# Down projections by Strassen's seven products between the up projections of a two-layer decoder trunk

## The chip, the cores and the metric

The kernel runs on one core of one Trainium2 chip. The metric is the device time of one execution in microseconds. The profiler gives one more execution, with the time of every instruction on every engine: TensorE (PE, and PEld for its weight loads), VectorE (DVE), ScalarE (ACT), GpSimd (POOL) and SyncE (SP, which here only issues transfers).

## The reference

A decoder trunk of two layers on 512 tokens of width 1024, in float32. Layer 0 has retention and stick-breaking attention, layer 1 differential attention. Behind each of them comes the part that this case is about, a gated MLP with a causal convolution of width 3 over the tokens:

```python
def conv_ffn(x, w_up, conv_w, conv_b, w_down):
    S = x.shape[1]
    h = x @ w_up                                   # 512 x 1024 by 1024 x 5632
    hp = jnp.pad(h, ((0, 0), (CONV_W - 1, 0), (0, 0)))
    h = sum(hp[:, j:j + S] * conv_w[j] for j in range(CONV_W)) + conv_b
    u, g = jnp.split(h, 2, axis=-1)
    return (jax.nn.silu(g) * u) @ w_down           # 512 x 2816 by 2816 x 1024
...
        f = conv_ffn(x, w_up[l], conv_w[l], conv_b[l], w_down[l])
        x = layer_norm(ALPHA * x + f, ln2_g[l], ln2_b[l])
```

## The kernel before

**Three matmuls for one.** Every float32 operand is kept as a pair of float32r tiles, a rounded one (`h`) and the rest (`l`). `mm3` (L138 to L142) computes h.h, h.l and l.h into one PSUM bank, so each 128 x 128 by 128 x 512 block product is three matmuls.

**Weights.** `wload` (L123) takes a chunk of 128 x 2048 values (1 MB): a transfer issued by SP into a `raw` tile (L126), two ScalarE copies of 1024 columns that round to `h` (L133) and two VectorE subtractions that leave `l` (L135). There are two raw buffers, and in the MLP five pairs of weight tiles in a ring (three of pool `w`, two of `ffnw`). `chunk` hands out the next chunk and calls for those `ahead` of it.

**The MLP of one layer** (`ffn`, L382). Of 5632 columns of `w_up`, 128 of u and the matching 128 of g are one chunk. An up projection is 2 x 8 x 3 = 48 matmuls into two banks, one for u and one for g, both [128 columns, 512 tokens]. `conv` (L396) then does the convolution: one ScalarE instruction (L400) and two VectorE ones (L402) per bank, SiLU on ScalarE (L407), the product u.g on VectorE (L408), and `act_split` (L328, L329) makes the pair of operand tiles of that block. There are 22 blocks per layer. The down projection takes them in groups of 8, 8 and 6 (`FFN_GROUPS`). The first two groups each run as one section: for each half of the 1024 output columns and each of four token blocks, 8 x 3 = 24 matmuls into one bank, which VectorE folds into the residual x (L468 in the first group, L471 in the second). The last group's banks go to the layer norm (`LayerNorm.add`, L918).

**PSUM** has eight banks: in the MLP six take matmul sums in turn (three of `mmps`, three of `mmps2`), two (`trps`) take transposes.

**Order.** TensorE runs its instructions in the order in which the program writes them. On the other engines, SP among them, a list scheduler sets the order when the program is built, and each engine then works its queue in that order. The last chunks of one stage and the first of the next share the ring. In the attention stages the order of TensorE's work is written out by hand (`EVEN_SEQ`, `EVEN_CUTS` and their like).

## Time and profile before

| | |
|---|---|
| Time, median of 3 runs | 1249.89 us (1249.67 to 1249.92) |
| Profiled execution, first to last instruction (its span) | 1247.3 us |
| Busy on TensorE, matmuls | 1223.3 us, 5972 matmuls |
| Busy on VectorE | 746.8 us, 1172 instructions |
| Busy on ScalarE | 543.0 us, 830 instructions |
| Busy on GpSimd | 84.7 us, 142 instructions |
| Moved by transfers | 123.34 MB, mean 99 GB/s |

The profile gives the span of its execution; what lies around the span is not listed apart. The profile's page lists, in order, the busy time of each engine, the span in 40 slices, the transfer queues, the chain of work that ended last, the costliest groups of instructions and the transfers issued. Other views of the same trace list instructions in order of time, who waited for whom, and busy times by stretch. L126 is line 126 of the kernel.

### The profile page before, as it was taken

The page shows a single profiled execution, that of the slowest core. Times are in us where ns is not written, and L with a number is a line of the kernel's source. Part 1 is how long each engine was busy: PE and PEld are TensorE (multiplying, and loading weights), DVE is VectorE, ACT ScalarE, POOL GpSimd, SP SyncE. Part 2 cuts the span into 40 slices and gives each one's busy share as a digit, 9 for nine tenths or more (in the row PEclk, how much of TensorE's full clock was granted, in tenths as well). Part 3 has the DMA queues.
Part 4 walks back from the last instruction along what each step waited for, and adds up shares of the span by engine and source line. Part 5 has one row for each costly group of instructions (what it writes and reads, how often), then busy time and mean ns, then how long its engine had stood idle before and what let it go on. Part 6 is the DMA issues. An engine that isn't in the chain of part 4 may idle for free.

```text
span 1247.3 us, 14937 instructions
## 1 busy us (share of the span) xinstructions
PE 1223.3 (98%) x5972; PEld 1014.0 (81%) x5972; DVE 746.8 (60%) x1172; ACT 543.0 (44%) x830; POOL 84.7 (7%) x142
## 2 busy tenths in 40 slices
PE   8999998999999999999999999999999999999997
PEld 6888877888888888888888888787988888888886
DVE  5866688796553466335565658777765445543544
ACT  5454565445441344223235658764544224422321
POOL 0211122110000000000000001011000000000000
PEclk9999999999999999999999999999999999999999
DMA  8322121243222222222152213222422132221201
GB/s 316 124 102 76 43 89 64 90 169 128 84 99 101 102 101 101 80 90 101 37 165 102 75 52 111 85 75 107 169 102 101 68 135 90 81 100 68 101 1 68
DMA packets 23565, 123.34 MB, mean 99 GB/s; under 512 B 3318, under 2 KB 4127, under 8 KB 10952
## 3 DMA queue, kind: packets, MB, share of 16 engines
q1 hardware_dynamic: 23496, 122.39, 27.6%
q8 instruction: 47, 0.77, 0.2%
q14 instruction: 22, 0.18, 0.0%
HBM read 120.26 MB, written 4.74 MB: 100 GB/s over the span
## 4 chain that ended last, share of the span: by engine, by line
PE 86%; DVE 6%; ACT 4%; issue 1%; POOL 1%; DMA 1%; POOLq 0%; DVEq 0%; ACTq 0%
PE mmps L141 26%; PE mmps L140 26%; PE mmps L142 26%; DVE wl L135 2%; PE dacc L837 1%; DVE t L586 1%; PE dz L321 1%; PE dz L320 1%; DVE t L584 1%; PE wtr L827 1%; PE sbacc L616 1%; PE mmps L650 1%; PE xtp L955 1%; ACT wh L133 1%; POOL zp L589 1%
## 5 line engine op out<-in xcount | busy, mean ns | idle before, releaser
L140 PE MATMUL mmps<-xTh,wh 128*128 128x512 f32 (+1 forms) x1008 | 384.5, 381 | 5.0 <-ACT wh L201 4.5
L141 PE MATMUL mmps<-xTl,wh 128*128 128x512 f32 (+1 forms) x1008 | 380.8, 378 | 0.8 <-DVE xTl L958 0.8
L142 PE MATMUL mmps<-xTh,wl 128*128 128x512 f32 (+1 forms) x1008 | 379.3, 376 | 0.5 <-DVE wl L135 0.5
L135 DVE TENSOR_TENSOR wl<-raw,wh 128x1024 fp32r<-128x1024 f32 x196 | 242.9, 1256 | 172.5 <-ACT wh L133 172.2
L133 ACT CAST wh<-raw 128x1024 fp32r<-128x1024 f32 x196 | 200.6, 1046 | 255.4 <-PE mmps L141 173.1
L140 PEld LDWEIGHTS mmps<-xTh,wh 128*128 128x128 f32 x1008 | 189.9, 188 | 39.7 <-ACT wh L201 4.5
L142 PEld LDWEIGHTS mmps<-xTh,wl 128*128 128x128 f32 x1008 | 189.7, 188 | 36.9 <-DVE wl L135 1.0
L141 PEld LDWEIGHTS mmps<-xTl,wh 128*128 128x128 f32 x1008 | 190.0, 188 | 33.6 <-DVE xTl L958 1.5
L140 PE MATMUL mmps<-wh,acth 128*128 128x512 f32 x480 | 191.1, 398 | 0.2
L141 PE MATMUL mmps<-wl,acth 128*128 128x512 f32 x480 | 188.2, 392 | 0.0
L142 PE MATMUL mmps<-wh,actl 128*128 128x512 f32 x480 | 188.0, 392 | 0.0
L402 DVE SCALAR_TENSOR_TENSOR cvt<-mmps,cv,cvt 128x511 f32<-128x511 f32 (+1 forms) x176 | 130.9, 745 | 40.2 <-ACT cvt L400 39.7
L140 PEld LDWEIGHTS mmps<-wh,acth 128*128 128x128 f32 x480 | 90.1, 188 | 21.2 <-DVE x L255 0.7
L142 PEld LDWEIGHTS mmps<-wh,actl 128*128 128x128 f32 x480 | 90.0, 188 | 21.0 <-DVE actl L332 0.5
L141 PEld LDWEIGHTS mmps<-wl,acth 128*128 128x128 f32 x480 | 90.1, 188 | 18.4
L400 ACT ACTIVATE cvt<-mmps,cv 128x512 f32<-128x512 f32 x88 | 68.3, 776 | 43.6 <-PE mmps L142 43.4
L407 ACT ACTIVATE cvt<-cvt 128x512 f32<-128x512 f32 x44 | 27.8, 632 | 85.9 <-DVE cvt L402 85.9
L140 PE MATMUL mmps<-wh,xTh 128*128 128x512 f32 x160 | 64.9, 406 | 0.0
L142 PE MATMUL mmps<-wh,xTl 128*128 128x512 f32 x160 | 62.6, 391 | 0.0
L141 PE MATMUL mmps<-wl,xTh 128*128 128x512 f32 x160 | 62.4, 390 | 0.0
L935 POOL TENSOR_SCALAR lst<-lst 128x1 f32<-128x1 f32 x16 | 7.1, 445 | 778.9 <-ACT junk L931 778.9
L328 ACT CAST acth<-cvt 128x512 fp32r<-128x512 f32 x44 | 26.9, 611 | 63.4 <-PE mmps L141 60.3
(142 smaller groups left out, 1163.7 us busy)
## 6 DMA issues: line engine op xcount, KB each, us to landing
raw<-in_w_up SPq DMA_DIRECT2D x44, 1024.0 KB, 4.8
raw<-in_w_down SPq DMA_DIRECT2D x22, 1024.0 KB, 4.8
raw<-in_w_ot SPq DMA_DIRECT2D x8, 1024.0 KB, 5.1
raw<-in_w_et SPq DMA_DIRECT2D x6, 1024.0 KB, 4.8
raw<-in_w_en SPq DMA_DIRECT2D x6, 1024.0 KB, 5.1
raw<-in_w_oe SPq DMA_DIRECT2D x4, 1024.0 KB, 5.4
raw<-in_w_on SPq DMA_DIRECT2D x4, 1024.0 KB, 4.8
raw<-in_w_oo SPq DMA_DIRECT2D x4, 1024.0 KB, 4.7
```

The costliest lines, as they stand in the source:

```text
L133: nc.scalar.copy(h[:, sl], raw[:, sl])
L135: nc.vector.tensor_tensor(l[:, sl], raw[:, sl], h[:, sl].bitcast(F32), op=ALU.subtract)
L140: mm(out, lh, rh, start=start, stop=False)
L141: mm(out, lh, rl, start=False, stop=False)
L142: mm(out, ll, rh, start=False, stop=stop)
L320: self.nc.tensor.matmul(out, lhs, B[:, m, 0:n], start=True, stop=False)
L321: self.nc.tensor.matmul(out, lhs, B[:, 2 + m, 0:n], start=False, stop=True)
L328: nc.scalar.copy(h, src)
L400: nc.scalar.activation(t, ps, AF.Identity, bias=cv[:, f, 3:4], scale=cv[:, f, 2:3])
L402: nc.vector.scalar_tensor_tensor(out=t[:, d:], in0=ps[:, :S - d], scalar=cv[:, f, c:c + 1], in1=t[:, d:], op0=ALU.mult, op1=ALU.add)
L407: nc.scalar.activation(g, g, AF.Silu)
L584: nc.vector.scalar_tensor_tensor(out=t, in0=zp, scalar=0.0, in1=t, op0=ALU.max, op1=ALU.add)
```

## The change

The first 16 blocks of a layer are taken in four groups of four. A group's part of the down projection is [512 tokens x 512] by [512 x 1024]. Each operand is cut into 2 x 2 parts (256 tokens by 256 of the inner dimension; 256 of the inner dimension by 512 columns), and the eight part products become seven, m1 to m7, each 2 token blocks x 2 x 3 = 12 matmuls of 512 columns. Four products need sums of two, three or four parts of the weights: SP loads the first part into the raw tile, and GpSimd issues transfers that add the others to it in memory. The sums of activations are four GpSimd subtractions of 256 columns per pair of blocks (`quad_operands`). The products stand between the next group's up projections (`SLOTS`): m1 and m2 behind the first, m5 and m6, m3 and m7, m4. Each sum stays in a PSUM bank to which the next product adds, and VectorE folds it into x, with either sign, at each step. The last six blocks stay as they were.

For this the weights of the whole kernel are handled in units of 1024 columns (512 KB) instead of 2048: four raw buffers (five in the MLP), six pairs of weight tiles (eight in the MLP). The MLP's up projections get four PSUM banks instead of six; the other two hold sums of the products, and two more of these lie in the banks of the transposes.

```diff
-FFN_GROUPS = ((0, 8), (8, 8), (16, 6))
+UNIT = 1024
+QUADS = 4
+LAST0 = 4 * QUADS
+LASTN = NPAIR - LAST0
+SUMS = {"m1": ("11",), "m2": ("21",), "m5": ("11", "12"), "m6": ("11", "12", "22"), "m3": ("22",), "m7": ("12", "22"),
+        "m4": ("11", "12", "21", "22")}
+BLOCKS = ("11", "12", "21", "22")
+SLOTS = (("m1", "m2"), ("m5", "m6"), ("m3", "m7"), ("m4",))
...
+    def unit(self, srcs):
+
         nc = self.nc
-        raw = self.rawp.tile([P, 2048], F32, tag="raw", name=self.nm("raw"))
-        nc.sync.dma_start(out=raw, in_=src)
+        raw = self.rawpools[self.ri % len(self.rawpools)].tile([P, UNIT], F32, tag="raw", name=self.nm("raw"))
+        self.ri += 1
+        nc.sync.dma_start(out=raw, in_=srcs[0])
+        for src in srcs[1:]:
+            nc.gpsimd.dma_start(out=raw, in_=src, accum_op=ALU.add)
+        h, l = self.unit_tiles()
+        nc.scalar.copy(h, raw)
+        nc.vector.tensor_tensor(l, raw, h.bitcast(F32), op=ALU.subtract)
+        return h, l
...
+    def unit_tiles(self):
         wp = self.wpools[self.wi % len(self.wpools)]
         self.wi += 1
-        h = wp.tile([P, 2048], F32R, tag="wh", name=self.nm("wh"))
-        l = wp.tile([P, 2048], F32R, tag="wl", name=self.nm("wl"))
-        halves = (slice(0, 1024), slice(1024, 2048))
-        for sl in halves:
-            nc.scalar.copy(h[:, sl], raw[:, sl])
-        for sl in halves:
-            nc.vector.tensor_tensor(l[:, sl], raw[:, sl], h[:, sl].bitcast(F32), op=ALU.subtract)
-        return h, l
-
-    def mm3(self, out, lh, ll, rh, rl, start, stop):
+        return (wp.tile([P, UNIT], F32R, tag="wh", name=self.nm("wh")),
+                wp.tile([P, UNIT], F32R, tag="wl", name=self.nm("wl")))
...
-        while self.csrc and len(self.cget) < ahead:
+        while self.csrc and sum(len(c.units) for c in self.cget.values()) < ahead:
             k = self.csrc.pop(0)
             self.cget[k] = self.wsrc(k)
 
     def wsrc(self, key):
+        if key[0] == "w_sum":
+            _, l, g, name = key
+            return Chunk([self.unit([self.a["w_quad"][l][g][BLOCKS.index(b)] for b in SUMS[name]])])
...
-        return self.wload(src)
+        return Chunk([self.unit([src[:, o:o + UNIT]]) for o in (0, UNIT)])
...
-        self.rawp = P_("raw", 2)
-        self.wp = P_("w", 3)
+        self.rawp = P_("raw", 4)
+        self.wp = P_("w", 6)
...
-            ps2 = c2.enter_context(self.pool(f"mmps2_{l}", 3, space=PSUM))
+            ps2 = c2.enter_context(self.pool(f"mmps2_{l}", 1, space=PSUM))
             tp = c2.enter_context(self.pool(f"ffnt_{l}", 2))
             cp = c2.enter_context(self.pool(f"ffnc_{l}", 1))
             w2 = c2.enter_context(self.pool(f"ffnw_{l}", 2))
+            act2 = c2.enter_context(self.pool(f"ffna_{l}", 4))
+            raw2 = c2.enter_context(self.pool(f"ffnr_{l}", 1))
             cv = cp.tile([P, 2 * NPAIR, 4], F32, tag="cv", name=self.nm("cv"))
             nc.sync.dma_start(out=cv, in_=self.a["conv"][l])
-            self.mmpools = [(self.mmps1, "mm"), (ps2, "mm2")]
-            self.wpools = [self.wp, w2, self.wp, w2, self.wp]
-            self.wi = 0
-            acts = {}
+            self.mmpools = [(self.mmps1, "mm")] * 3 + [(ps2, "mm2")]
+            self.mmi = 0
+            self.wpools = [self.wp, self.wp, self.wp, w2] * 2
+            self.rawpools = [self.rawp] * 4 + [raw2]
+            self.wi = self.ri = 0
+            acts, firsts, ops = {}, {}, {}
+            t1, t2 = slice(0, 256), slice(256, S)
+
+            def quad_operands(g, kk, u, v):
+
+                q = tp.tile([P, 4, 256], F32, tag="q", name=self.nm("q"), bufs=1)
+                sub = nc.gpsimd.tensor_tensor
+                sub(q[:, 0], u[:, t2], v[:, t2], op=ALU.subtract)
+                sub(q[:, 3], u[:, t2], u[:, t1], op=ALU.subtract)
+                sub(q[:, 1], u[:, t1], q[:, 0], op=ALU.subtract)
+                sub(q[:, 2], v[:, t1], q[:, 1], op=ALU.subtract)
+                ah = act2.tile([P, S], F32R, tag="a2", name=self.nm("ah"))
+                al = act2.tile([P, S], F32R, tag="a2", name=self.nm("al"))
+                nc.scalar.activation(ah[:, t1], u[:, t1], AF.Copy, scale=-1.0)
+                nc.scalar.copy(ah[:, t2], v[:, t1])
+                nc.vector.scalar_tensor_tensor(out=al[:, t1], in0=u[:, t1], scalar=-1.0, in1=ah[:, t1].bitcast(F32),
+                                               op0=ALU.mult, op1=ALU.subtract)
+                nc.vector.tensor_tensor(al[:, t2], v[:, t1], ah[:, t2].bitcast(F32), op=ALU.subtract)
+                a = self.actp.tile([P, S], F32R, tag="act", name=self.nm("a22"))
+                nc.scalar.activation(a[:, t1], v[:, t2], AF.Copy, scale=-1.0)
+                nc.vector.scalar_tensor_tensor(out=a[:, t2], in0=v[:, t2], scalar=-1.0, in1=a[:, t1].bitcast(F32),
+                                               op0=ALU.mult, op1=ALU.subtract)
+                qs = [self.act_split(q[:, i:i + 2].rearrange("p a b -> p (a b)")) for i in (0, 2)]
+                for name, (h, l_), o in (("m1", (ah, al), 0), ("m2", (ah, al), 256), ("m5", qs[0], 0), ("m6", qs[0], 256),
+                                         ("m3", qs[1], 0), ("m7", qs[1], 256)):
+                    ops[g, name, kk] = (h[:, o:o + 256], l_[:, o:o + 256])
+                ops[g, "m4", kk] = (a[:, t1], a[:, t2])
 
             def conv(i, pu, pg):
                 hs = []
                 for ps, f in ((pu, i), (pg, NPAIR + i)):
-                    t = tp.tile([P, S], F32, tag="cu" if f == i else "cg", name=self.nm("cvt"))
+                    tag, n = ("cu", 3) if f == i else ("cg", 2)
...
-                acts[i] = self.act_split(u)
-
-            full, lo, hi = slice(0, S), slice(0, 256), slice(256, S)
+                if i >= LAST0:
+                    acts[i] = self.act_split(u)
+                elif i % 2 == 0:
+                    firsts[i] = u
+                else:
+                    quad_operands(i // 4, i % 4 // 2, firsts.pop(i - 1), u)
+
+            full = slice(0, S)
+            slots = {}
+            for g in range(QUADS):
+                at = [4 * g + 4 + j for j in range(4)] if g + 1 < QUADS else [LAST0 + j for j in (1, 2, 4, 5)]
+                for i, names in zip(at, SLOTS):
+                    slots[i] = [(g, name) for name in names]
...
+            for i in range(NPAIR):
+                keys += [("w_up", l, i)] + [("w_sum", l, g, name) for g, name in slots.get(i, ())]
+            dk = [("w_down", l, i) for i in range(LASTN // 2)]
+            self.csrc, self.cget = keys + dk, {}
+            self.prefetch(4)
...
+            banks, touched = {}, set()
+
+            def update(ps, tb, half, sign):
+                xs = self.x[:, tb, half * S:(half + 1) * S]
+                op = ALU.add if sign > 0 else ALU.subtract
+                if (tb, half) in touched:
+                    nc.vector.tensor_tensor(xs, xs, ps, op=op)
+                else:
+                    touched.add((tb, half))
+                    nc.vector.scalar_tensor_tensor(out=xs, in0=xs, scalar=ALPHA, in1=ps, op0=ALU.mult, op1=op)
+
+            def product(g, name):
+
+                w = self.chunk(("w_sum", l, g, name), 4)
+                for tau in range(2):
+                    if name == "m1":
+                        banks["e", tau] = ps2.tile([P, S], F32, tag="e", name=self.nm("wine"), bufs=2)
+                    elif name in ("m2", "m5"):
+                        banks["c", tau] = self.trps.tile([P, S], F32, tag="tr", name=self.nm("winc"))
+                    ps = banks["e" if name in ("m1", "m6", "m7", "m4") else "c", tau]
+                    first = name in ("m1", "m2", "m5")
+                    ts = slice(tau * P, (tau + 1) * P)
+                    for kk in range(2):
+                        h, l_ = ops[g, name, kk]
+                        self.mm3(ps, h[:, ts], l_[:, ts], *w.get(kk * S, S), first and kk == 0, kk == 1,
+                                 skip_group_check=not first)
+                    lo, hi = tau, 2 + tau
+                    for tb, half, sign in {"m1": ((lo, 0, -1),), "m2": ((lo, 0, 1),), "m5": ((hi, 1, 1),),
+                                           "m6": ((lo, 1, 1),), "m3": ((lo, 1, 1),), "m7": ((hi, 1, 1),),
+                                           "m4": ((hi, 0, -1),)}[name]:
+                        update(ps, tb, half, sign)
+
+            for i in range(2, NPAIR):
+                up(i)
+                for g, name in slots.get(i, ()):
+                    product(g, name)
...
+class Chunk:
+
+
+    def __init__(self, units):
+        self.units = units
+
+    def get(self, at, n):
+        h, l = self.units[at // UNIT]
+        sl = slice(at % UNIT, at % UNIT + n)
+        return h[:, sl], l[:, sl]
```

## Rows read from the trace of the kernel before

**Rows 1.** The page: busy time of each engine, and the granted clock in 40 slices.

```profile
PE 1223.3 (98%) x5972; PEld 1014.0 (81%) x5972; DVE 746.8 (60%) x1172; ACT 543.0 (44%) x830; POOL 84.7 (7%) x142
...
PEclk9999999999999999999999999999999999999999
```

**Rows 2.** Busy times by stretch; us, busy us (instructions) per engine, clock, DMA share, GB/s.

```profile
core 0: us, PE busy (x) PEld busy (x) DVE busy (x) ACT busy (x) POOL busy (x), PEclk, DMA share, GB/s
0.00:284.00 284.00, 271.46 (x1484) 224.55 (x1485) 204.72 (x319) 144.69 (x204) 52.21 (x46) 1.00 0.34 122
284.00:658.00 374.00, 374.00 (x1694) 308.12 (x1693) 196.81 (x255) 131.71 (x170) 3.97 (x8) 1.00 0.27 96
658.00:904.00 246.00, 242.18 (x1330) 205.90 (x1329) 172.21 (x375) 156.02 (x314) 25.56 (x80) 1.00 0.28 98
904.00:1247.30 343.30, 335.66 (x1470) 275.45 (x1468) 173.03 (x224) 110.53 (x143) 2.93 (x8) 1.00 0.23 83
```

**Rows 3.** Single lines, layer 0: duration ns min/median/max, first and last start us.

```profile
L468 DVE SCALAR_TENSOR_TENSOR x<-x,mmps x8: 680/686/689, 376.4 to 415.0; 128x512 f32<-128x512 f32 x8
...
L471 DVE TENSOR_TENSOR x<-x,mmps x8: 677/686/689, 507.7 to 546.7; 128x512 f32<-128x512 f32 x8
```

**Rows 4.** Timeline of ScalarE in layer 0's MLP: start us, us, instruction [idle before].

```profile
304.66 1.05 ACT L133 CAST wh<-raw 128x1024 fp32r<-128x1024 f32 x1 [3.92 <-PE mmps L141]
...
315.65 1.05 ACT L133 CAST wh<-raw 128x1024 fp32r<-128x1024 f32 x1 [3.98 <-PE mmps L141]
...
326.53 1.05 ACT L133 CAST wh<-raw 128x1024 fp32r<-128x1024 f32 x1 [3.92 <-PE mmps L141]
```

**Rows 5.** Waits of SP: for whom, us in total, times, longest us.

```profile
SPq L126 <- DVE wl L135: 888.4, 88, 23.4
```

**Rows 6.** Timeline of SP in layer 0's MLP.

```profile
308.79 0.33 SPq L126 DMA_DIRECT2D raw<-in_w_down  x1
```

**Rows 7.** Groups of VectorE, 284 to 658 us: busy us, mean ns | idle before.

```profile
L135 DVE TENSOR_TENSOR wl<-raw,wh 128x1024 fp32r<-128x1024 f32 x62 | 74.9, 1219 | 80.3 <-ACT wh L133 80.3
L402 DVE SCALAR_TENSOR_TENSOR cvt<-mmps,cv,cvt 128x511 f32<-128x511 f32 x88 | 65.5, 745 | 18.1 <-ACT cvt L400 17.9
L408 DVE TENSOR_TENSOR cvt<-cvt,cvt 128x512 f32<-128x512 f32 x22 | 15.2, 692 | 15.8 <-ACT cvt L407 15.8
L329 DVE TENSOR_TENSOR actl<-cvt,acth 128x512 fp32r<-128x512 f32 x22 | 15.0, 684 | 2.2 <-ACT acth L328 2.2
...
L468 DVE SCALAR_TENSOR_TENSOR x<-x,mmps 128x512 f32<-128x512 f32 x8 | 5.5, 685 | 20.7 <-PE mmps L142 20.7
```

**Rows 8.** A single line of VectorE with 256 columns, whole span.

```profile
L578 DVE TENSOR_TENSOR zp<-z,sbmask x8: 406/411/415, 69.5 to 231.1; 128x256 f32<-128x256 f32 x8
```

**Rows 9.** Timeline of VectorE in layer 0's MLP.

```profile
295.89 1.53 DVE L402 SCALAR_TENSOR_TENSOR cvt<-mmps,cv,cvt 128x511 f32<-128x511 f32 x2
...
321.17 0.69 DVE L408 TENSOR_TENSOR cvt<-cvt,cvt 128x512 f32<-128x512 f32 x1 [0.76 <-ACT cvt L407]
```

**Rows 10.** Groups of ScalarE, 284 to 658 us.

```profile
L133 ACT CAST wh<-raw 128x1024 fp32r<-128x1024 f32 x62 | 63.9, 1046 | 114.4 <-PE mmps L141 78.5 <-PE mmps L142 35.8
...
L328 ACT CAST acth<-cvt 128x512 fp32r<-128x512 f32 x22 | 13.4, 611 | 31.7 <-PE mmps L141 30.2 <-DVE cvt L408 1.5
```

**Rows 11.** Single lines of GpSimd, whole span: min/median/max ns, first and last start.

```profile
L589 POOL TENSOR_TENSOR zp<-zp,t x16: 1532/1564/2632, 53.9 to 237.5; 128x640 f32<-128x640 f32 x16
...
L558 POOL TENSOR_TENSOR rt<-rt,t x8: 1283/1301/2329, 33.0 to 207.3; 128x512 f32<-128x512 f32 x8
```

**Rows 12.** Transfers issued: queue, count, KB each, median us to landing.

```profile
raw<-in_w_down SPq DMA_DIRECT2D x22, 1024.0 KB, 4.8
...
x<-in_x SPq DMA_DIRECT2D x4, 512.0 KB, 7.7
...
cs<-in_c_cs SPq DMA_DIRECT2D x1, 512.0 KB, 9.1
```

**Rows 13.** Timeline of VectorE and GpSimd in layer 0's attention.

```profile
62.68 2.60 DVE L135 TENSOR_TENSOR wl<-raw,wh 128x1024 fp32r<-128x1024 f32 x1
...
61.79 2.40 POOL L589 TENSOR_TENSOR zp<-zp,t 128x640 f32<-128x640 f32 x1 [6.37 <-DVE t L586]
```

More of the change, by code (lines that the diff above doesn't have):

```diff
@@ L154, in chunks, with chunk @@
             self.csrc += [(src, first + n * i + j) for j in range(n)]
-    def chunk(self, key, ahead=1):
+    def chunk(self, key, ahead=2):
         n = self.csrc.index(key) if key in self.csrc else -1
@@ L190, in start_proj @@
             nc.sync.dma_start(out=xr[:, a * S:b * S], in_=x_in[:, a * S:b * S])
-            for (wr, _, _), src in zip(ws, srcs):
+            for (wr, _), src in zip(ws, srcs):
                 nc.sync.dma_start(out=wr[:, vl], in_=src[:, vl])
@@ L194, in start_proj @@
             if kk == KT - 1:
-                self.prefetch(1)
+                self.prefetch(2)
             gl = slice(kk * S, (kk + 1) * S)
             nc.scalar.copy(xh[:, gl], xr[:, gl])
-            for i, (wr, wh, wl) in enumerate(ws):
+            for i, (wr, w) in enumerate(ws):
                 if kk in cuts:
                     vl = slice(kk * 256, cuts[kk] * 256)
-                    nc.scalar.copy(wh[:, vl], wr[:, vl])
+                    wh, wl = w.get(vl.start, vl.stop - vl.start)
+                    nc.scalar.copy(wh, wr[:, vl])
                 if i == 0:
@@ L245, in g_out0 @@
         for half in range(2):
-            wh, wl = ws[half]
             for tb in range(TB):
@@ L250, in g_out0 @@
                 for i, (ah, al) in enumerate(acts):
-                    sl = slice(i * S, (i + 1) * S)
-                    self.mm3(ps, ah[:, ts], al[:, ts], wh[:, sl], wl[:, sl], i == 0, i == 3)
+                    self.mm3(ps, ah[:, ts], al[:, ts], *ws[half].get(i * S, S), i == 0, i == 3)
                     yield MM
@@ L260, in out1_mm @@
         ts = slice(tb * P, (tb + 1) * P)
-        wh, wl = self.ws1[i // 2]
-        sl = slice((i % 2) * DM + half * S, (i % 2) * DM + half * S + S)
-        self.mm3(ps, act[0][:, ts], act[1][:, ts], wh[:, sl], wl[:, sl], i == 0, i == 3)
+        w = self.ws1[i // 2].get(i % 2 * DM + half * S, S)
+        self.mm3(ps, act[0][:, ts], act[1][:, ts], *w, i == 0, i == 3)
     def g_out1a(self, wn, y):
@@ L398, in conv @@
                 for ps, f in ((pu, i), (pg, NPAIR + i)):
-                    t = tp.tile([P, S], F32, tag="cu" if f == i else "cg", name=self.nm("cvt"))
+                    tag, n = ("cu", 3) if f == i else ("cg", 2)
+                    t = tp.tile([P, S], F32, tag=tag, name=self.nm("cvt"), bufs=n)
                     nc.scalar.activation(t, ps, AF.Identity, bias=cv[:, f, 3:4], scale=cv[:, f, 2:3])
@@ L431, in up @@
             def up(i):
-                w = self.chunk(("w_up", l, i), 2)
+                w = self.chunk(("w_up", l, i), 4)
                 pss = [self.mmps(), self.mmps()]
@@ new lines, in ffn, with down_mm @@
+            for i in range(2, NPAIR):
+                up(i)
+                for g, name in slots.get(i, ()):
+                    product(g, name)
+            def down_mm(ps, tb, half, i):
+                ts = slice(tb * P, (tb + 1) * P)
+                ah, al = acts[LAST0 + i]
+                self.mm3(ps, ah[:, ts], al[:, ts], *ws[i // 2].get(i % 2 * DM + half * S, S), i == 0, i == LASTN - 1)
+            ws = [self.chunk(k, 0) for k in dk]
+            ln2 = LayerNorm(self, 2, l, l + 1 < DEPTH)
@@ new lines, in ffn @@
+            if l == 0:
+                bias_ps = self.bias_tables()
+            first = [self.mmps(), self.mmps()]
+            for half in range(2):
+                for i in range(LASTN - 1):
+                    down_mm(first[half], 0, half, i)
+            for u in range(8):
+                tb, half = u // 2, u % 2
+                if u < 2:
+                    ps = first[u]
+                    down_mm(ps, 0, half, LASTN - 1)
+                else:
+                    ps = self.mmps()
+                    for i in range(LASTN):
+                        down_mm(ps, tb, half, i)
+                ln2.add(tb, half, ps)
+                if u == 5 and l == 0:
+                    bias_ps()
+                if u in (4, 6) and l + 1 < DEPTH:
+                    ln2.transpose(u // 2 - 2)
@@ L929, in norm @@
                                 op0=ALU.add, op1=ALU.mult)
-        junk = b.gbp.tile([P, DM], mybir.dt.bfloat16, tag="junk", name=b.nm("junk"))
+        junk = b.gbp.tile([P, DM], mybir.dt.bfloat16, tag="junk", name=b.nm("junk"), bufs=1)
         nc.scalar.activation(junk, x, AF.Square, bias=st[:, 0:1], accum_out=st[:, 1:2])
@@ L985, in _chunk_o, with _quads @@
     return np.stack(res)
+def _quads(w):
+    r = _rows(w)
+    cut = lambda g, k, n: r[:, 4 * g + k:4 * g + 4:2, n * S:(n + 1) * S].reshape(P, -1)
+    return np.stack([np.stack([cut(g, int(b[0]) - 1, int(b[1]) - 1) for b in BLOCKS]) for g in range(QUADS)])
 def _constants():
@@ L1031 @@
                           for l in range(DEPTH)]),
-        "w_down": np.stack([_chunk_o(i["w_down"][l], [tuple(range(p0, p0 + n)) for p0, n in FFN_GROUPS])
-                            for l in range(DEPTH)]),
+        "w_quad": np.stack([_quads(i["w_down"][l]) for l in range(DEPTH)]),
+        "w_down": np.stack([_chunk_o(i["w_down"][l], [tuple(range(LAST0, NPAIR))]) for l in range(DEPTH)]),
         "conv": conv.reshape(DEPTH, 4, 2 * NPAIR, P).transpose(0, 3, 2, 1),
```

101 lines of the change are left out of this document (16 added, 85 removed).

## The prediction

> **What bounds the kernel now.** I read the page's busy shares first. TensorE is busy 98% of the span, VectorE 60%, ScalarE 44%, GpSimd 7%, and the granted clock is in the top tenth in all 40 slices, so TensorE runs at its 2.4 GHz level throughout [rows 1]. A share over the whole span mixes stages, so I cut the span at the stages' borders [rows 2]. The MLP stages are the second and the fourth stretch. In the second TensorE is busy 374.00 of 374.00 us; in the fourth it misses 7.6 us, most of them behind the last matmul. There a matmul less is its own time less, as long as nothing new makes TensorE wait.
>
> What one matmul costs is not its listed duration, since matmuls overlap. I take the step. In the first long down section VectorE folds a bank into x after every 24 matmuls: eight such instructions from 376.4 to 415.0, so 38.6 / (7 x 24) = 0.230 us; in the second section 39.0 / 168 = 0.232 [rows 3]. Up projections step a little faster: ScalarE's next weight copy is released by the end of an up projection at 315.65 and again at 326.53, so 48 matmuls took 10.88 us, 0.227 each [rows 4].
>
> Then I ask how early weights come. SP spends 888.4 us in 88 waits for VectorE to finish a split and so free a raw buffer [rows 5]. The first down chunk, tenth in the order (nine up chunks stand before it), is issued at 308.79 [rows 6], when TensorE has just ended the third up projection at 304.66 [rows 4]. Ten less three is seven: five pairs of weight tiles and two raw buffers. Lookahead is thus set by buffers, not by the place of the call. The same reading serves below.
>
> **Matmuls.** A group of four blocks takes 2 halves x 4 token blocks x 4 x 3 = 96 matmuls before and 7 products x 2 x 2 x 3 = 84 after. Four groups in two layers: 96 fewer, at 0.231 us (between the two down steps) 22.2 us. Priced at the up step it is 21.8, at the slower down step 22.3. The shapes stay 128x512, and I count nothing else for them.
>
> **VectorE, per layer.** Weights: a group has 4 units before and 7 after, so 12 more splits at 1.219 us [rows 7] = 14.6. Updates of x: 14 per group instead of 16 per layer, 40 more at 0.685 [rows 7] = 27.4. Operands: a pair of blocks keeps two 512-wide splits and gains three 256-wide ones, 0.411 from the nearest row of that width [rows 8], so 8 x 1.23 = 9.9. Sum 52: from 196.8 to about 249 in a stage of 374 - 11 = 363 us, 69%. In the busiest repeat (four up projections and seven products, 4 x 10.9 + 84 x 0.231 = 63.0 us) it is 15 splits 18.3, convolutions 4 x (4 x 0.745 + 0.692) = 14.7, operands 5.2, updates 9.6: 47.8, or 76%.
>
> What is queued behind that? A bank goes on accumulating only after its update. The shortest distance from a bank's last matmul to its next use is one up projection, 10.9 us, against about 1.4 for two updates. The tightest is m1 of a layer's first group: its operands come from up projection 3, and only up projection 4 lies between, 10.9 us. Convolution now runs from the end of an up projection at 315.65 [rows 4] to 321.17 + 0.69 [rows 9], 6.2 us; two 256-wide copies (at most 0.611 each, the 512-wide copy [rows 10]) and two splits add 2.0. That leaves 2.7 us; in later groups m4 adds 2.8. I put 1 us per layer for the first group and 0.5 over all the others; the bounds are 0 and 2.7 per group, 0 to 22 us.
>
> **ScalarE** gains 12 copies at 1.046 [rows 10] and 24 half copies of at most 0.611: 27 us on 131.7, 44% of the stage. Its queue is in order, and what stands behind a copy are the convolutions; they have the 10.9 us of the other pair of banks. Nothing.
>
> **PSUM.** Up projections get four banks instead of six. The hardest place is the stage's start; there the fourth bank of the first two up projections is released at 295.89 + 1.53 = 297.4 [rows 9], and up projection 3 starts at 304.66 [rows 4]. Nothing, with 7 us of cover.
>
> **GpSimd's arithmetic.** Eight 256-wide subtractions per group. The nearest rows are 1.301 us for 512 and 1.564 for 640 columns [rows 11], which give 0.78 for 256: 25 us per layer on an engine that has 4 [rows 2]. m5 needs them about 30 us after the up projection that feeds them. Their own time is hidden; what they do to VectorE is a rival below.
>
> **The accumulating transfers.** Seven per group, issued by GpSimd, each behind the landing of the one before on its tile; m4 chains three. No row shows one. Below I take 4.8 us, a plain load of twice the bytes; above 9.1, the slowest plain 512 KB, and twice that, 18.2, if reading the target costs a second pass [rows 12]. I take 7.7, the row of the same size beside other traffic [rows 12]. Now the cover: with eight weight pairs and five raw buffers of one unit each, the load of unit n may start when TensorE has ended unit n - 13. For m4, behind up projection 7, that is up projection 4, and 49 us of matmuls lie between (three up projections and six products). Less two splits (3.5), the load (4.8) and its own split (2.3) 38.6 us are left for three transfers: 12.9 each. At 7.7 there are 15 us to spare. m6 chains two and m7 one. GpSimd's queue is in order, so behind m4's chain its subtractions may stand 15 us; of the 30 us they have, convolution, subtractions and splits take 12. Nothing, but without much to spare.
>
> **Traffic, SP and the rest.** Three more loads and seven accumulates per group, 5 MB, make 20 MB per layer against 96 GB/s x 374 us = 36 MB now, at a DMA share of 0.27 [rows 2]: well below full. SP issues 78 loads per layer instead of 33 at 0.33 us [rows 6], 15 us of a queue that mostly waits [rows 5]. The last six blocks are as before, with m4 as extra cover for the last convolution. In the attention stages only the halved units are new: TensorE is idle 12.5 and 3.8 us there [rows 2]; a finer release may help or a shifted order hurt, 0 with 2 us either way.
>
> **Sum.** 22.2 - 2.5 = 19.7 us. The profiled span of 1247.3 us becomes 1227.6. The median of the runs shown is 1249.9, 2.6 us above the span; I add the same: 1230.
>
> **Rivals.** *VectorE becomes late.* When GpSimd's 640-wide instruction ran beside a split, it took 2.40 instead of 1.56, and the split 2.60 instead of 1.22 [rows 11, 13]. If each of the eight subtractions costs VectorE 1.38 us, the 63 us of a group hold 47.8 + 11.0 = 58.8 us, 93%, in an in-order queue that also waits for ScalarE. Then the 2.7 us of cover at m1 is gone and banks come late. At 1 to 2 us for each of eight groups, 8 to 16 us come back: 1236 to 1246. Against it: a 256-wide instruction is 0.78 long, and only splits with both inputs in SBUF met it. The Trainium skill, page "SBUF — State Buffer", section "SBUF: two separate sides", says that VectorE and GpSimd share a port pair under an exclusive lock and that the loser blocks for a whole instruction. The overlap in the trace agrees.
>
> *The chain of m4 ends last.* Its place is m4 behind the fourth up projection, its price three transfers in a row, and it decides from 12.9 us each. Every us beyond costs 3 x 8 = 24 us, so at 13.7 the gain is gone, and at 15 us the time is 1230 + 50 = 1280. For it: nothing here has measured such a transfer, and my upper bound lies beyond. Against it: every plain 512 KB landed within 9.1 us.
>
> *The attention stages lose.* Their hand-set order was matched to whole chunks. If TensorE's 16.3 idle us there grow by half, 8 us: 1238. Nothing in the rows asks for it, since few of their waits are for weights. That the change does not remove what it says has no chance: the count is in the loops.
>
> **How the numbers follow.** Forecast 0.60 (1226 to 1235 with the bounds of its small terms), VectorE late 0.22, m4's chain 0.12, attention 0.06. A measurement of this kernel tells 0.2%, 2.5 us, from no change. The first, second and fourth case are faster save 0.04 in their upper tails; the third is slower. The range of 1226 to 1246 takes in the forecast and the two milder rivals and leaves out the chain.
>
> **What would show it.** Right: 448 instead of 480 matmuls on each of the three lines with an activation as weights, TensorE without idle time in the MLP stages, these some 10 us shorter each. Wrong in VectorE: TensorE waiting for operands or for an update of x at the start of products, with VectorE above 85% there. Wrong in the chain: ScalarE waiting for a raw tile at m4, and TensorE behind it; transfers above 13 us. A time above 1246 would make the prediction wrong, whatever the cause.

## The result, and the profile after

The changed kernel takes 1257.51 us, the median of four runs (1255.54 to 1258.5), beside 1249.91 of the kernel before on the same chip: a ratio of 1.0059, 95% interval 1.0044 to 1.0073. It is 0.6% slower, where 1230 was forecast and 1246 was the upper end of the range. The profiled execution took 1257.86 us with a span of 1255.7.

The page of the kernel after, busy time and granted clock, against [rows 1]:

```profile
PE 1211.5 (96%) x5876; PEld 1001.0 (80%) x5876; DVE 845.3 (67%) x1324; ACT 580.9 (46%) x902; POOL 195.9 (16%) x262
...
PEclk9999999999999989999999999999999999999998
```

The 96 matmuls are gone (5876 instead of 5972), but TensorE's busy time fell by 11.8 us and not by 22, and its idle time rose from 24.0 to 44.2. The clock's top tenth is left in two slices.

To see where, I cut both spans at TensorE's own marks: its first transposition for the MLP of layer 0, the second one for the next stage behind that MLP, the first for the MLP of layer 1, the end. Busy times by stretch, columns as in [rows 2], first the kernel before, then the kernel after:

```profile
0.00:260.65 260.65, 248.84 (x1321) 203.69 (x1322) 185.14 (x293) 133.58 (x188) 48.92 (x42) 1.00 0.33 117
260.65:632.18 371.53, 370.80 (x1732) 307.34 (x1730) 201.75 (x258) 132.48 (x172) 5.78 (x10) 1.00 0.26 94
632.18:865.23 233.05, 231.08 (x1188) 193.40 (x1187) 157.20 (x359) 145.49 (x302) 24.57 (x78) 1.00 0.30 103
865.23:1247.30 382.07, 372.57 (x1737) 309.59 (x1735) 202.68 (x263) 131.41 (x171) 5.39 (x13) 1.00 0.25 89
```

```profile
0.00:264.95 264.95, 250.49 (x1320) 205.29 (x1321) 181.74 (x292) 133.31 (x186) 48.38 (x41) 0.99 0.34 116
264.95:634.79 369.84, 362.54 (x1684) 299.80 (x1683) 251.78 (x334) 151.26 (x208) 61.30 (x72) 0.99 0.56 149
634.79:873.31 238.52, 233.00 (x1188) 193.18 (x1186) 158.69 (x360) 145.85 (x301) 25.33 (x78) 1.00 0.32 103
873.31:1255.70 382.39, 365.45 (x1689) 302.70 (x1687) 253.11 (x340) 150.45 (x207) 60.86 (x72) 0.98 0.54 143
```

The four stages changed by +4.3, -1.7, +5.5 and +0.3 us, together +8.4. So two things went wrong at once: both attention stages, which hold no new arithmetic, are longer, and the MLP stages, which lost 11.1 us of matmuls each, give nearly nothing. In the MLP stages idle time of TensorE grew from 0.7 to 7.3 and from 9.5 to 16.9 us, and its matmuls cost more at a mean granted clock of 0.99 and 0.98.

VectorE's load came out as forecast. The stretch of [rows 2] from 284 to 658 us, in the kernel after:

```profile
284.00:658.00 374.00, 366.11 (x1659) 300.93 (x1658) 250.56 (x334) 153.13 (x210) 58.10 (x68) 0.99 0.58 155
```

It is busy 250.56 us (forecast 249, before 196.81 [rows 2]), 67%, so it is not what TensorE waits for by sheer work. The waits say more. Waits of the kernel after: engine and line, for whom, us in total, times, longest us:

```profile
ACT wh L139 <- DMA raw<-in_w_quad: 176.5, 18, 18.3
...
PE winc L151 <- ACT ah L416: 7.6, 3, 4.1
PE wine L151 <- DVE x L487: 5.3, 3, 2.3
```

In the MLP stages TensorE waits mostly for operands (ah) and for updates of x, never for the summed weights themselves. ScalarE's weight copies, which waited for TensorE before, now stand 176.5 us in 18 waits for a summed unit to land. Yet the transfers are no slower than I took them to be. Issues of the kernel after, KB each, median us to landing, beside [rows 12]:

```profile
raw<-in_w_quad SPq DMA_DIRECT2D x56, 512.0 KB, 4.5
raw<-in_w_quad POOLq DMA_DIRECT2D x56, 512.0 KB, 6.2
```

6.2 us for an accumulating transfer of 512 KB; I had taken 7.7. What a chain (a load and the accumulating transfers behind it on the same tile) does shows at the first m4 of layer 0. Timeline of the kernel after, rows of SP, GpSimd, ScalarE, VectorE and TensorE (start us, us, instruction, idle before it and what ended it):

```profile
333.36 0.33 SPq L135 DMA_DIRECT2D raw<-in_w_quad  x1
...
338.88 0.88 POOL L137 DMA_DIRECT2D raw<-in_w_quad  x1 [9.81 <-DVE wl L140]
...
347.25 0.88 POOL L137 DMA_DIRECT2D raw<-in_w_quad  x1 [6.41 <-DMA raw<-in_w_quad]
353.83 0.87 POOL L137 DMA_DIRECT2D raw<-in_w_quad  x1 [5.71 <-DMA raw<-in_w_quad]
...
348.37 0.78 ACT L435 ACTIVATE cvt<-mmps,cv 128x512 f32<-128x512 f32 x1
359.59 1.05 ACT L139 CAST wh<-raw 128x1024 fp32r<-128x1024 f32 x1 [10.44 <-DMA raw<-in_w_quad]
360.55 0.62 ACT L442 ACTIVATE cvt<-cvt 128x512 f32<-128x512 f32 x1
...
392.90 1.05 ACT L139 CAST wh<-raw 128x1024 fp32r<-128x1024 f32 x1 [10.91 <-DMA raw<-in_w_quad]
...
429.07 1.05 ACT L139 CAST wh<-raw 128x1024 fp32r<-128x1024 f32 x1 [17.00 <-DMA raw<-in_w_quad]
...
361.20 0.69 DVE L443 TENSOR_TENSOR cvt<-cvt,cvt 128x512 f32<-128x512 f32 x1 [8.37 <-ACT cvt L442]
...
380.28 0.39 PE L151 MATMUL wine<-wh,a 128*128 128x512 f32 x1
```

SP issues the load of m4's first block at 333.36. GpSimd issues the three accumulating transfers one behind the other at 338.88, 347.25 and 353.83; the sum is there at 359.5. TensorE uses it at 380.28, 20 us later: for TensorE the chain is early. But ScalarE's queue holds the rounding copy of that unit in front of the SiLU (L442) of a convolution, and its turn came at 349.15. It stands 10.44 us; the SiLU, VectorE's product behind it (8.37 us idle) and the operands of the next products are late behind it. In the second group the copy of m6, a chain of two, waits 10.91 us (from 382) and that of m4 17.00 (from 412); over all eight groups m4's copy waits 10.4 us in the first and 13.8 to 18.3 in the others. From 430 on TensorE begins to run out of work. Busy times of the kernel after in windows of 10 us, columns as in [rows 2]:

```profile
420.00:430.00 10.00, 10.00 (x46) 8.26 (x45) 0.00 (x0) 0.93 (x1) 0.87 (x1) 1.00 0.52 91
430.00:440.00 10.00, 8.95 (x40) 7.02 (x39) 9.28 (x12) 7.63 (x12) 3.13 (x3) 1.00 0.31 105
...
460.00:470.00 10.00, 5.87 (x18) 4.31 (x17) 5.53 (x8) 5.17 (x9) 3.18 (x4) 0.70 0.65 139
```

From 420 to 430 VectorE does nothing at all while TensorE still has work; TensorE's gaps follow. The larger one lasts 4.13 us, to 465.91, and the granted clock of the window at 460 is 0.70: a mean of its two levels of 1.2 and 2.4 GHz, since it fell to the lower one at 463.92 (lines in the last section).

### The profile page after: what moved, and what is told of

Same layout as the page of the kernel before. It is cut to its first block, busy times and chain, and to the rows that moved or that the text cites. A ratio compares the mean times of both kernels' runs of the same rounds, so it can differ in the third digit from the quotient of the medians.

```text
span 1255.7 us, 15600 instructions
## 1 busy us (share of the span) xinstructions
PE 1211.5 (96%) x5876; PEld 1001.0 (80%) x5876; DVE 845.3 (67%) x1324; ACT 580.9 (46%) x902; POOL 195.9 (16%) x262
## 2 busy tenths in 40 slices
DMA packets 49202, 165.33 MB, mean 132 GB/s; under 512 B 6166, under 2 KB 6975, under 8 KB 49128
## 3 DMA queue, kind: packets, MB, share of 16 engines
q1 hardware_dynamic: 41064, 134.98, 32.6%
q0 software_dynamic: 8064, 29.36, 13.5%
## 4 chain that ended last, share of the span: by engine, by line
PE 52%; DMA 18%; DVE 17%; ACT 6%; issue 5%; POOL 2%; POOLq 0%; DVEq 0%; ACTq 0%
DMA raw<-in_w_quad 17%; PE mmps L151 14%; PE mmps L152 14%; PE mmps L153 14%; DVE wl L140 6%; DVE cvt L437 2%; ACT wh L139 2%; PE dacc L888 1%; DVE actl L332 1%; DVE x L487 1%; DVE t L637 1%; PE wine L151 1%; DVE cvt L443 1%; PE wine L152 1%; PE wine L153 1%
## 5 line engine op out<-in xcount | busy, mean ns | idle before, releaser
L140 DVE TENSOR_TENSOR wl<-raw,wh 128x1024 fp32r<-128x1024 f32 x220 | 270.4, 1241 | 104.9 <-ACT wh L139 103.9
L139 ACT CAST wh<-raw 128x1024 fp32r<-128x1024 f32 x220 | 226.7, 1045 | 245.3 <-DMA raw<-in_w_quad 176.5
L153 PEld LDWEIGHTS mmps<-xTh,wl 128*128 128x128 f32 x1008 | 190.4, 189 | 36.8 <-DVE wl L140 1.0
L437 DVE SCALAR_TENSOR_TENSOR cvt<-mmps,cv,cvt 128x511 f32<-128x511 f32 (+1 forms) x176 | 131.0, 745 | 12.9 <-ACT cvt L435 11.1
L137 POOL DMA_DIRECT2D raw<-in_w_quad x56 | 49.3, 881 | 398.0 <-DMA raw<-in_w_quad 252.7
L151 PE MATMUL mmps<-wh,acth 128*128 128x512 f32 x224 | 91.5, 408 | 2.5 <-ACT acth L331 1.2
L153 PE MATMUL mmps<-wh,actl 128*128 128x512 f32 x224 | 88.5, 395 | 0.1
L152 PE MATMUL mmps<-wl,acth 128*128 128x512 f32 x224 | 88.2, 394 | 0.0
L443 DVE TENSOR_TENSOR cvt<-cvt,cvt 128x512 f32<-128x512 f32 x44 | 30.2, 687 | 83.6 <-ACT cvt L442 83.6
L442 ACT ACTIVATE cvt<-cvt 128x512 f32<-128x512 f32 x44 | 27.7, 631 | 85.1 <-DVE cvt L437 85.1
L151 PEld LDWEIGHTS mmps<-wh,acth 128*128 128x128 f32 x224 | 42.4, 189 | 13.0 <-DVE x L262 1.9
L153 PEld LDWEIGHTS mmps<-wh,actl 128*128 128x128 f32 x224 | 42.3, 189 | 10.2 <-DVE actl L335 0.5
L152 PEld LDWEIGHTS mmps<-wl,acth 128*128 128x128 f32 x224 | 42.5, 190 | 7.6
```

The costliest lines, as they stand in the source:

```text
L137: nc.gpsimd.dma_start(out=raw, in_=src, accum_op=ALU.add)
L139: nc.scalar.copy(h, raw)
L140: nc.vector.tensor_tensor(l, raw, h.bitcast(F32), op=ALU.subtract)
L151: mm(out, lh, rh, start=start, stop=False, **kw)
L152: mm(out, lh, rl, start=False, stop=False, **kw)
L153: mm(out, ll, rh, start=False, stop=stop, **kw)
```

## The experiments

Theory A: the chain of a summed unit, with ScalarE's in-order copy in front of the convolutions, stops ScalarE. Rivals: B, the traffic; C, VectorE's added work and GpSimd's subtractions beside it. Later theory U: the attention stages lose by the half-size units. Ratios are to the kernel before on the same chip, with the 95% interval in brackets; in_w_quad is the tensor of the parts that the products' weights are summed from.

**Without sums.** SUMS names one block for each product: `"m5": ("11",), "m6": ("11",), "m7": ("12",), "m4": ("11",)`.

> Every product takes one block of the down weights in place of the sum: no accumulating transfer is issued, all else stays (the sums of weights are left out). Theory A (the unit of a long chain of accumulating transfers lands late, and ScalarE's in-order queue, with the copy of that unit in front of the convolutions, stops): the gain of 96 matmuls appears, 1228 to 1233 us, ratio to before 0.982 to 0.987, and ScalarE's waits for in_w_quad fall from 176.5 us to under 30. Rival B (too much traffic): the same, since 28 MB are gone with the chain. Rival C (VectorE's 52 us per layer, and GpSimd's subtractions beside it): still over 1248 us, with TensorE waiting for operands and updates as now.

Measured 1237.35 us, ratio 0.9898 [0.9881, 0.9914]; ScalarE has no wait for in_w_quad left. 20 us come back, so it is the sums, or their traffic as B has it; but 1237 is 4 us above what A expected, and the missing part lies in the attention stages (265.1 and 239.5 us).

**The same transfers, aside.**
```
-            nc.gpsimd.dma_start(out=raw, in_=src, accum_op=ALU.add)
+            side = self.dramp.tile([P, UNIT], F32, name=self.nm("side"))
+            nc.gpsimd.dma_start(out=side, in_=src)
```

> As the run without sums, but every accumulating transfer is replaced by a plain one of the same 512 KB, from the same block, on the same GpSimd queue, into memory that nobody reads (the sums of weights are left out): the transfers stay, nobody waits for them. Theory A: 1228 to 1236 us, within 4 us of the run without sums. Rival B (traffic, DMA engines full in these stretches): 1248 us or more, plain loads of weights slower than 8 us. Rival C: over 1248 us as well, but without late loads.

Measured 1275.68 us, 1.0209 [1.0182, 1.0236]. It tells nothing on the question, since with nobody to wait for, the 56 transfers were all issued in the first 128.2 us. Its busy times by stretch, columns as before:

```profile
0.00:284.00 284.00, 238.74 (x1226) 195.01 (x1227) 169.31 (x270) 127.48 (x178) 73.63 (x94) 0.97 0.59 201
284.00:658.00 374.00, 372.75 (x1761) 309.78 (x1759) 267.25 (x353) 162.74 (x216) 34.08 (x44) 1.00 0.36 116
```

The start is starved (DMA share 0.59), and the MLP behind it runs without its traffic (0.36). The run with nine raw buffers answers B instead.

**Without subtractions.** The four `sub(...)` lines, run twice per group, go; `qs = [self.act_split(t) for t in (u, v)]`.

> GpSimd's eight subtractions per group are left out; the operands of m5, m6, m3 and m7 are split from the two blocks themselves (these four products get wrong operands); all chains stay. Theory A: little changes, 1249 to 1258 us, ScalarE still waits over 130 us for in_w_quad. Rival C in its form of the shared port (each subtraction costs VectorE about 1 us, and operands come late): 1228 to 1240 us.

Measured 1246.12 us, 0.9969 [0.9957, 0.998]: between the theories. ScalarE's waits for in_w_quad stay (181.3 us), yet 11 us come back.

**Nine raw buffers.**
```
-            w2 = c2.enter_context(self.pool(f"ffnw_{l}", 2))
...
-            raw2 = c2.enter_context(self.pool(f"ffnr_{l}", 1))
+            raw2 = c2.enter_context(self.pool(f"ffnr_{l}", 5))
...
-            self.wpools = [self.wp, self.wp, self.wp, w2] * 2
-            self.rawpools = [self.rawp] * 4 + [raw2]
+            self.rawpools = [self.rawp] * 4 + [raw2] * 5
```

> Nine raw buffers in place of five, paid for by two pairs of weight tiles (six in place of eight); the computation is whole. Theory A: loads may run nine units, some 47 us, ahead of a copy instead of five units, 26 us, so a chain of 26 us is hidden: 1228 to 1238 us, ScalarE's waits for in_w_quad under 60 us. Rival B: no gain, 1250 us or more. Rival C: no gain, 1250 us or more.

Measured 1235.82 us, 0.9882 [0.9868, 0.9897], with every transfer of the changed kernel (165.34 MB against 165.33). B is out. Timeline of this kernel at the same place, rows of SP, GpSimd and ScalarE, and below it ScalarE's waits:

```profile
322.95 0.33 SPq L135 DMA_DIRECT2D raw<-in_w_quad  x1
...
327.47 0.88 POOL L137 DMA_DIRECT2D raw<-in_w_quad  x1
...
333.24 0.88 POOL L137 DMA_DIRECT2D raw<-in_w_quad  x1 [4.12 <-DMA raw<-in_w_quad]
341.40 0.87 POOL L137 DMA_DIRECT2D raw<-in_w_quad  x1 [7.28 <-DMA raw<-in_w_quad]
...
361.47 1.05 ACT L139 CAST wh<-raw 128x1024 fp32r<-128x1024 f32 x1 [1.71 <-PE mmps L152]
```

```profile
ACT wh L139 <- PE mmps L152: 134.7, 87, 7.8
...
ACT wh L139 <- DMA raw<-in_w_quad: 1.7, 1, 1.7
```

m4's load starts at 322.95 instead of 333.36, and the three transfers are as slow as before (the last lands at 348.8). m4's copy, at 361.47, waits for TensorE to free a weight tile, not for a landing; waits of ScalarE for a landing of in_w_quad come to 1.7 us in the whole run. ScalarE waits for TensorE again, as in the kernel before.

**m4's chain alone.** `"m4": ("11", "12")`.

> The changed kernel, but m4 takes the sum of two blocks instead of four, so its chain is one accumulating transfer instead of three (two blocks are left out of m4's sum); m5, m6 and m7 keep theirs. Theory A with the length of the chain deciding (load plus three transfers, 26 us, against some 26 us that five raw buffers give; m6 with two lies just within): most of the 20 us between the changed and the deep-raw kernel come back, 1238 to 1246 us. Rival (each accumulating transfer costs its share, 16 of 56 are gone): 1250 to 1253 us.

Measured 1235.69 us, 0.9887 [0.9872, 0.9902]: not most of the loss but as much as nine raw buffers give back. The orders of ScalarE and VectorE are the same, instruction for instruction, as in the changed kernel, so this is the cleanest pair. ScalarE at the same place, and TensorE's MLP stages:

```profile
348.71 0.78 ACT L435 ACTIVATE cvt<-mmps,cv 128x512 f32<-128x512 f32 x1
350.70 1.05 ACT L139 CAST wh<-raw 128x1024 fp32r<-128x1024 f32 x1 [1.21 <-PE winc L153]
352.07 0.63 ACT L442 ACTIVATE cvt<-cvt 128x512 f32<-128x512 f32 x1 [0.33 <-DVE cvt L437]
```

```profile
265.31:624.86 359.55, 358.72 (x1683) 298.58 (x1682) 259.52 (x334) 156.80 (x208) 52.89 (x64) 1.00 0.51 142
...
863.06:1232.60 369.54, 360.67 (x1689) 300.83 (x1687) 262.18 (x340) 156.20 (x207) 51.60 (x65) 1.00 0.49 137
```

The convolution, m4's copy (at 350.70) and the SiLU follow each other without a wait for a transfer, where the changed kernel stood until 359.59; the MLP stages are 10.3 and 12.9 us shorter than in the changed kernel. 40 of the 56 accumulating transfers are still there, chains of two for m6 among them, and cost little that shows: ScalarE waits 11.0 us for in_w_quad in the whole run.

**Nine raw buffers without subtractions.** The two edits above together.

> The deep-raw kernel without GpSimd's eight subtractions per group (m5, m6, m3 and m7 get wrong operands). Leaving them out of the changed kernel gave 11 us back. Theory A (they only hurt because convolutions that were late behind a chain made the next transfers late in GpSimd's queue, and that loop is gone with nine raw buffers): 1233 to 1236 us, under 3 us gained on 1235.8. Rival C (they cost VectorE time and TensorE waits by themselves): 1223 to 1228 us.

Measured 1235.65 us, 0.988 [0.9864, 0.9897], against 1235.82 with the subtractions. C is out: with the chains on time they cost nothing. The 11 us of the third run go with the late chains; that they come of the subtractions' place in GpSimd's queue behind a chain is my reading and not shown, since that run also has another order on ScalarE.

**m4's copy on GpSimd.** `if len(srcs) == 4: nc.gpsimd.tensor_copy(h, raw)`, else ScalarE as before.

> The changed kernel, but the rounding copy of m4's unit is made by GpSimd, whose queue waits for this chain anyway, instead of ScalarE. The computation is whole. Theory A1 (the stop is ScalarE's: the copy of m4's unit stands there in front of the convolution's SiLU): ScalarE's waits for in_w_quad fall from 176 to under 60 us and nearly all 20 us come back, 1235 to 1240 us. Theory A2 (GpSimd's subtractions and VectorE's operands stand behind the same chain, so that freeing one of three queues helps little): 1246 to 1258 us.

Measured 1247.98 us, 0.9985 [0.9976, 0.9994]: 9.5 of the 22 us come back, within A2's range. Waits of this kernel:

```profile
ACT acth L334 <- POOL q L414: 102.3, 16, 14.8
...
DVE wl L143 <- POOL wh L140: 86.5, 8, 15.4
...
ACT wh L142 <- DMA raw<-in_w_quad: 53.4, 10, 12.0
```

ScalarE's wait for the landing fell to 53.4 us as A1 asked, but it now waits 102.3 us (42.0 in the changed kernel) for GpSimd's subtractions, and VectorE 86.5 us for m4's copy. The chain stops three queues, each worked in its order; freeing one hands the wait to the next.

**Six raw buffers.** `ffnr` 2, `ffnw` 1, rings of 4 + 2 raw and 6 + 1 weight tiles.

> Six raw buffers instead of five, paid for by one pair of weight tiles (seven instead of eight). The computation is whole. At 374 us for 72 units a raw buffer more lets a load start 5.2 us earlier, 31 instead of 26 us ahead of its copy; m4's chain took 26 us with its load. Theory A with a threshold: most of the 20 us come back with this one buffer, 1235 to 1243 us. Rival (the loss falls evenly with the depth, a quarter of the way from five to nine): 1250 to 1254 us.

Measured 1235.53 us, 0.9885 [0.9871, 0.99]: all of it again, with one raw buffer more and one weight pair less. But not as I had written. SP and ScalarE at the same place:

```profile
332.77 0.33 SPq L135 DMA_DIRECT2D raw<-in_w_quad  x1
...
351.18 0.63 ACT L442 ACTIVATE cvt<-cvt 128x512 f32<-128x512 f32 x1 [0.31 <-DVE cvt L437]
356.97 1.05 ACT L139 CAST wh<-raw 128x1024 fp32r<-128x1024 f32 x1 [5.15 <-DMA raw<-in_w_quad]
```

The load starts no earlier (332.77 against 333.36), because raw and weight buffers together are still thirteen. The copy comes later: with a weight pair less it stands behind the SiLU, and its turn is at 351.81, 19.0 us from the load's start where the changed kernel has 15.8 (with nine raw buffers 36.8). That is still too short for the chain: m4's copy waits 5.15 us here and 3.7 to 11.7 in the other seven groups. It costs nothing that shows: TensorE is idle 10.6 us in the MLP stages, against 24.2 in the changed kernel and 9.7 with m4's chain short. So a wait of this length is not by itself the price. What differs is what stands behind the copy in ScalarE's queue: the SiLU there, none here.

Both runs with more raw buffers also have fewer weight pairs, and no run takes a weight pair away alone. Whether the raw buffer or the new order gave the 22 us back in this run is open.

**Units without Strassen.** The units and `Chunk` of the changed kernel and its rings in the attention stages; in the MLP four raw buffers and ten weight pairs, the bytes of the kernel before; the down projections of the kernel before.

> Half-size units (512 KB loads, four raw and six weight buffers of half the size) as in the changed kernel, but the down projections of the kernel before: no Strassen products, no sums, no accumulating transfers, all 96 matmuls back. In the runs so far the first transposition of the MLP of layer 0 starts at 265 us instead of 260.65, and the second attention stage (second transposition of layer 0's end to the first of layer 1) takes 239 to 240 us instead of 233.1, in all kernels with units. Theory U (the units alone cost the attention stages these 10.8 us, since the order on ScalarE and VectorE no longer fits TensorE's hand-set order): 1257 to 1263 us, both stages as in the changed kernel. Rival (it comes from the new MLP: its layout, its prefetches): 1248 to 1252 us, both stages as in the kernel before.

Measured 1259.5 us, 1.0075 [1.006, 1.009]; the stages are 265.4, 372.2, 239.0 and 381.4 us. Theory U holds: +4.7 and +5.9 in the attention stages, 0.7 and -0.6 in the MLP. The wait of TensorE that grew most in the first attention stage, before and in this run:

```profile
PE atr L600 <- DVE rS L644: 1.0, 1, 1.0
```

```profile
PE atr L596 <- DVE rS L640: 2.4, 1, 2.4
```

It is for VectorE and not for weights. TensorE's order in that stage is the same in both kernels, but at least 19 of ScalarE's 188 instructions and 23 of VectorE's 293 stand elsewhere in theirs.

**Whole chunks again.** Tiles of two units, one 1 MB load for a plain chunk; a tile of sums holds a slot's products; 4 raw and 3 weight tiles in the MLP.

> The deep-raw kernel with whole 1 MB chunks again: raw and weight tiles of two units (two raw and three weight tiles in the attention stages, as before the change; four raw and three weight tiles in the MLP), a tile of the MLP's sums holds m1 and m2, m5 and m6, m3 and m7, or m4. The computation is whole. Theory U with theory A: the attention stages return to 260.7 and 233 us, the MLP stages stay at 338 to 340 and 371, 1223 to 1229 us, ratio 0.979 to 0.983. Rival (the attention stages lose elsewhere): 1234 to 1238 us. Rival (four raw tiles are too coarse, chains are late again): attention as before the change, but TensorE idle in the MLP, 1230 to 1245 us.

Measured 1227.01 us, 0.9819 [0.9805, 0.9834]. Busy times by the same marks:

```profile
0.00:260.66 260.66, 248.79 (x1320) 203.68 (x1321) 182.79 (x291) 130.03 (x184) 48.92 (x42) 1.00 0.34 121
260.66:621.05 360.39, 357.93 (x1683) 298.77 (x1682) 255.24 (x334) 154.42 (x209) 57.80 (x70) 1.00 0.54 149
621.05:854.15 233.10, 230.92 (x1187) 193.37 (x1186) 156.82 (x358) 144.53 (x300) 25.19 (x78) 1.00 0.32 112
854.15:1225.20 371.05, 359.89 (x1688) 301.12 (x1688) 257.75 (x343) 154.45 (x209) 58.58 (x72) 0.99 0.52 145
```

The attention stages are back (260.66 and 233.10 against 260.65 and 233.05; in the first at most 4 of ScalarE's instructions and 2 of VectorE's stand elsewhere than before), the MLP stages 11.1 and 11.0 us shorter than before. This beats both kernels.

**Whole tiles, two loads each.** `for sl in halves: nc.sync.dma_start(out=raw[:, sl], in_=parts[0][0][:, sl])`.

> The whole-chunk kernel (1227.0 us), but each 1 MB chunk is loaded by two transfers of 512 KB into the halves of its tile; tiles, their release and the splits stay whole. The computation is whole. Theory U1 (the attention stages lose by tiles and splits of half size, which come free and are scheduled one by one): no change, 1225 to 1229 us, attention stages 260.7 and 233. Theory U2 (they lose by the smaller transfers): 1234 to 1238 us, attention stages 265 and 239.

Measured 1228.22 us, 0.9828 [0.9812, 0.9845]; stages 260.97, 360.53, 232.60. So it is not the smaller transfers. Nor is it the split instructions, which are 128x1024 in all these kernels. What is left is the tile of half size: two halves come free one by one, and the order on ScalarE and VectorE comes out another than the one that TensorE's hand-set order was made for. That the order is the cause fits the waits, but no run changes it alone, and which reordered instruction costs which microsecond was not tried.

## Why the prediction was wrong

**Matmuls: right.** 22.2 us were forecast from 96 x 0.231. The whole-chunk kernel's span is 1225.2 against 1247.3, 22.1 less.

**VectorE: right in size, its loss was not there.** Forecast +52 us a layer; by TensorE's marks the MLP of layer 0 has 251.78 against 201.75, +50.0, and 255.24 in the whole-chunk kernel, +53.5. The 2.5 us of losses do not show in the whole-chunk kernel, nor does the rival: GpSimd's subtractions cost nothing once the chains are on time.

**The transfers' price: right.** 6.2 us, taken 7.7, bounds 4.8 to 18.2. In m4's first chain the steps were 8.4, 6.6 and 5.7.

**The chain's cover: the first step that failed.** I reckoned that 49 us of matmuls lie between the start of m4's load and its use on TensorE. That held: 333.36 to 380.28 is 46.9. From that I took 12.9 us for each transfer and "decides from 12.9 us each". But the first to need the sum is ScalarE, which had its turn at 349.15. The first accumulating transfer was issued at 338.88, behind the load, so 10.3 us were left for three transfers, 3.4 each. At 6.9 they were 10 us late. The step as I wrote it under ScalarE was: "what stands behind a copy are the convolutions; they have the 10.9 us of the other pair of banks. Nothing." The first wait of 10.4 us is about that cover, but m4's copy waited 13.8 to 18.3 us in the other seven groups, and behind it GpSimd's subtractions and VectorE's splits were late too. That it was worth asking how long the copy itself may wait stood in the text, as "ScalarE waiting for a raw tile at m4", only as a sign of the rival. Price: 23.1 us by span between the changed kernel and the one with m4's chain short. The rival named the right place, with a chance of 0.12, but set its point of decision against TensorE's use, 12.9 us where ScalarE's turn left 3.4; by its own rule, transfers of 6.2 us cost nothing.

**The attention stages: the second.** "0 with 2 us either way", with a rival of 8 us at 0.06. Units alone cost 9.2 us by medians, 10.7 by span. The argument was that few of TensorE's waits there are for weights. True, and beside the point: what changed is the tile that comes free, and with it the order of other instructions on ScalarE and VectorE; TensorE's waits that grew are for those. The rival had the size about right (9.8 us in the two stages of the changed kernel), and its sign, more idle time of TensorE there: 13.8 us became 20.0. The rest is matmuls that took longer, in part at the lower clock (last section).

Together: the whole-chunk kernel, which shows neither loss, took 1227.0, 3 us under the forecast of 1230. With the units' 9.2 that makes 1236.2, where the kernel with nine raw buffers took 1235.8; with the 21.8 of m4's chain in full (1257.5 less 1235.7) it makes 1258.0, where the changed kernel took 1257.5.

## What to carry to other kernels

A buffer's lookahead has two parts: raw buffers cover the time from a load's start to its conversion, converted buffers the time from there to its use. A longer load draws on the first part, and the time it has ends at the turn of the first in-order queue that touches it, not at the use on TensorE. What a late load then costs depends on what stands behind it in that queue: the six-raw kernel waited up to 11.7 us there at no cost, the changed kernel 10.4 to 18.3 at 22 us in all. Where one engine's order is written by hand around what the others do, a change of tile size is a change of that order, and has to be priced stage by stage even where no arithmetic changes.

## What I had not expected of the hardware

Accumulating transfers into SBUF took longer than plain ones, but far less than my upper bound: 512 KB in 6.2 us median against 4.5 for the plain loads of the same tensor, and 7.2 against 3.6 in the kernel with nine raw buffers. They also held the 16 DMA engines longer. In the changed kernel the packets of GpSimd's queue took 13.5% of the engines' span for 29.36 MB, those of the plain queue 32.6% for 134.98 MB: 1.9 times as long per byte. No plain transfer ran from GpSimd's queue into SBUF, so what is due to the queue and what to the adding is open. Issuing one takes 0.88 us of GpSimd's time (56 take 49.3 us). In a chain on one tile the next starts only behind the landing of the last; the Trainium skill, page "DMA: Bandwidth & Descriptors", section "Rules for kernel authors", asks for just that wait, because an accumulate reads its target and writes it later. All chains here keep it, so no run shows what happens without.

A few microseconds of idle TensorE cost more than themselves: between the changed kernel and the one with m4's chain short, idle time in the MLP stages differs by 14.5 us (7.30 + 16.94 against 0.83 + 8.87), and the same matmuls are 8.6 us longer (362.54 + 365.45 against 358.72 + 360.67). The granted clock tells why in part. Three stretches of the changed kernel's MLP stages in which TensorE has work, columns as in [rows 2]:

```profile
463.92:470.74 6.82, 4.83 (x11) 3.76 (x12) 5.95 (x9) 4.50 (x9) 2.31 (x3) 0.50 0.39 109
1044.18:1047.60 3.42, 3.42 (x9) 2.65 (x9) 3.42 (x5) 2.27 (x4) 1.66 (x2) 0.50 0.48 158
1112.45:1115.86 3.41, 3.41 (x8) 2.73 (x9) 3.41 (x4) 1.47 (x4) 2.49 (x3) 0.50 0.29 65
```

There the clock stood at 0.50, the level of 1.2 GHz; each fall came during or within 1 us behind an idle stretch of TensorE, of 4.13, 2.33 and 1.90 us. The kernel with m4's chain short has no such stretch in its MLP stages while TensorE works. TensorE is busy 11.66 us in the three; at the full clock that would be half, so an estimated 5.8 of the 8.6 us are the clock's, and the other 2.8 stay open. The changed kernel has one more in its first attention stage, 3.41 us from 218.16, which the kernel before and the whole-chunk kernel do not have. Not every gap does it: 2.06 us of idle time before 1076.55 had no fall behind them.
